# Seven block products in place of eight in the first MLP product of a transformer layer

## The chip, the cores and the metric

The kernel runs on one core of one Trainium2 chip. The metric is the time of one execution on the device in microseconds. The core has five engines with instruction queues of their own: TensorE (PE, matmuls, with its weight loads shown as PEld), VectorE (DVE), ScalarE (ACT), GpSimd (POOL), and SyncE (SP), which here issues all DMAs. SBUF is the memory that the engines work in, PSUM the one that TensorE accumulates in, in eight banks of 512 fp32 columns by 128 partitions.

## The reference

One layer of a diffusion backbone on 512 latent tokens and 256 context tokens of width 1024, in fp32. After two mixers (windowed attention and a gated DeltaNet) and their output projection comes the MLP, and the change is in it:

```python
def mlp(s, shift, scale_m):
    hm = rms_norm(s, g_norm2) * (1.0 + scale_m) + shift
    return jnp.square(jax.nn.relu(hm @ w_mlp1)) @ w_mlp2

x_new = x.astype(jnp.float32) + gt1 * merge(y_attn, o_dl, dz, ga, gd)
x_new = x_new + gt2 * mlp(x_new, sh2, sc2)
```

`w_mlp1` is 1024 x 4096, `w_mlp2` is 4096 x 1024; `hm` has 512 rows (tokens) and 1024 columns.

## The kernel before

Everything is kept transposed: 128 features on the partitions, tokens along the free axis. Each fp32 operand of a matmul is split in two parts of the type fp32r, `hi` (the rounded value) and `lo` (the rest). A product of two such operands takes three matmuls per 128x128 weight block, hi x hi, hi x lo and lo x hi, which `mm3` issues (lines 294, 295, 296). The split is one ACT copy and one DVE subtraction: `split` (lines 182 and 183) for values on the chip, `wload` (lines 240, 245, 246) for weights that it first loads from memory to a `wr` tile (four of them, 512 KB each).

The MLP works in four quarters (`for hf in range(4)`). A quarter computes eight tiles of 128 features of the first product, each from eight 128x128 weight blocks with all 512 tokens as the moving operand (24 matmuls of 512 columns, line 1380), then relu (ACT, line 1382), square (DVE, line 1384) and split (lines 182, 183). Then the second product takes the quarter's eight tiles as its input: for each of eight output tiles 24 matmuls, and DVE adds the gated result to the residual stream `xn_` in SBUF (line 1401). In the last quarter each output tile is stored at once (line 1405). The first three tiles of the first quarter are computed in two halves of 256 tokens, since the norm ahead of the MLP is done by halves (`norm`, `modulate`, lines 299 to 301).

Beside the first quarter's eight tiles the DVE has other work: steps of `late_mod` (lines 1037 to 1042), which load a piece of the modulation weights and reduce it (one instruction of 1024 columns each).

Buffers: `alloc` hands out pieces of one SBUF arena of 167 units of 256 columns in a ring, one after the other, and goes on from where it stopped; `free` returns a piece, and its next owner has to wait until the last reader is done. `keep=True` takes a piece from the top end. Weights of the MLP lie in the arena (`bufs = [alloc(1024), alloc(1024)]`), in the profile `m`; other weights lie in the two rotating pairs of tiles `wh` and `wl`. PSUM banks are handed out by `bank()` in the same way.

A scheduler orders the instructions of each engine when the program is built; it takes the order of the program as a priority and puts a later instruction ahead where an earlier one isn't ready by its own estimate.

Of the kernel before, what the change touches and what calls it, by code (L numbers as in the profile page):

```python
# [11 lines left out]
AF = mybir.ActivationFunctionType  # L12
ALU = mybir.AluOpType
# [17 lines left out]
NPL = ()  # L31
# [3 lines left out]
P = 128  # L35
D = 1024
KT = D // P
# [24 lines left out]
class Buf:  # L62


    def __init__(self, arena, start, n, ap):
        self.arena, self.start, self.n, self.ap = arena, start, n, ap

    def __getitem__(self, k):
        return self.ap[k]

    def free(self):
        for i in range(self.start, self.start + self.n):
# [25 lines left out]
def tile_layer(ctx: ExitStack, tc: tile.TileContext, I: dict, out: bass.AP, dbg=None):  # L98
    nc = tc.nc
    V, A, G, PE = nc.vector, nc.scalar, nc.gpsimd, nc.tensor  # L100
# [19 lines left out]
    alloc, bank = mem.get, lambda n=1: banks.get(n * 512)  # L120
# [10 lines left out]
    r32 = lambda ap: ap.bitcast(F32R)  # L131
    f32_ = lambda ap: ap.bitcast(F32)
# [5 lines left out]
    def act(out_, in_, func, **kw):  # L138

        sets = TABLES.get(func)  # L140
        if sets and actg["set"] not in sets:
            head = A.preload_act_table_set(sets[0])
            for o in actg["ops"]:
                tc.add_manual_dep(head.ins, o.name, nosync, reason="table sets")
            actg.update(set=sets[0], head=head.ins, ops=[head.ins])
        r = A.activation(out_, in_, func, **kw)  # L146
        if sets:
            tc.add_manual_dep(r.ins, actg["head"].name, nosync, reason="table sets")
            actg["ops"].append(r.ins)
        return r  # L150
# [87 lines left out]
    def wload(src, n=KT, bufs=None):  # L238
        raw = sb.tile([P, KT, P], F32, tag="wr", bufs=NWR, name=nm("wr"))[:, :n]
        nc.sync.dma_start(out=raw, in_=src)  # L240
        if bufs:
            hi, lo = (b.ap.rearrange("p (k c) -> p k c", k=KT) for b in bufs)
        else:
            hi, lo = (sb.tile([P, KT, P], F32, tag=t, bufs=NWS, name=nm(t))[:, :n] for t in ("wh", "wl"))
        A.activation(r32(hi), raw, AF.Copy)  # L245
        V.tensor_tensor(r32(lo), raw, hi, op=ALU.subtract)  # L246
        return r32(hi), r32(lo)
# [16 lines left out]
    rx, rc = rstd[:, :512], rstd[:, 512:768]  # L264

    for src, nt, n, r in ((xs_, 4, SEQ, rx), (cs_, 2, CTX, rc)):
        tot = None
        for i in range(nt):
            b = alloc(1024)
# [6 lines left out]
        w = 512  # L276
# [12 lines left out]
    def mm3(acc, w, xs, start=True, stop=True, ks=None):  # L289
        ks = list(range(len(xs))) if ks is None else ks  # L290
        n = len(ks)
        for i, k in enumerate(ks):
            xhi, xlo = xs[i]
            PE.matmul(acc, w[0][:, k, :], xhi, start=(start and i == 0), stop=False)  # L294
            PE.matmul(acc, w[0][:, k, :], xlo, start=False, stop=False)  # L295
            PE.matmul(acc, w[1][:, k, :], xhi, start=False, stop=(stop and i == n - 1))  # L296

    def modulate(t, src, r, sc, sh, hi, lo, eng=V):
        V.scalar_tensor_tensor(t, src, sc, r, op0=ALU.mult, op1=ALU.mult)
        A.activation(r32(hi), t, AF.Identity, bias=sh)  # L300
        eng.scalar_tensor_tensor(r32(lo), t, sh, hi, op0=ALU.add, op1=ALU.subtract)
        return r32(hi), r32(lo)
# [6 lines left out]
    for kt in range(KT):  # L309
        t = alloc(768)  # L310
        o, oc = kt * 1024, kt * 512
# [325 lines left out]
    acc = in_tile(T_AB, True)  # L637
    V.memset(gb[0:64], 0.0)

    t, t2 = alloc(TOK), alloc(TOK)  # L640
# [390 lines left out]
    modT = const.tile([P, 4, 8], F32, name="modT")  # L1031
# [13 lines left out]
    late = (x for grp in range(4) for x in late_mod(grp))  # L1045
# [154 lines left out]
    for g in range(2):  # L1200
        ms = slice(16 * g, 16 * g + 16)
# [11 lines left out]
        for a in range(2):  # L1213
            lo, hi = quad(a, 0), quad(a, 1)
# [36 lines left out]
    for qq in range(2):  # L1251
# [3 lines left out]
        for a in range(2):  # L1255
            n = 2 * qq + a
            t = alloc(512)
# [15 lines left out]
    for ct in range(8):  # L1273
        w = wnext()
# [32 lines left out]
    for ct in range(8 - NHALF):  # L1307
        w = wnext()
# [9 lines left out]
    HM = alloc(8 * 1024, True)  # L1318
    ms = [(r32(HM[:, k * 1024:k * 1024 + 512]), r32(HM[:, k * 1024 + 512:k * 1024 + 1024])) for k in range(KT)]

    wlast = [wnext() for _ in range(NHALF)]
    accs = [bank() for _ in range(NHALF)]
    wfirst = []

    def norm(cols):
# [4 lines left out]
        act(rx[:, cols], rx[:, cols], AF.Exp, scale=-0.5)  # L1330
        for kt in range(KT):
            t = alloc(256)
            modulate(t.ap, xn_[kt][:, cols], rx[:, cols], mA[:, kt:kt + 1], modT[:, 1, kt:kt + 1],
                     f32_(ms[kt][0][:, cols]), f32_(ms[kt][1][:, cols]),
                     G if kt in NPL else V)
            t.free()

    first = []

# [7 lines left out]
    for n, cols in enumerate(halves):  # L1347
        for i in range(NHALF):
            if n and i == NHALF - 1:
                norm(halves[0])  # L1350
            mm3(accs[i][:, cols], wlast[i], cut(ys, cols))
            residual(8 - NHALF + i, accs[i], cols)
    for b in accs:
# [4 lines left out]
        f.append(bank())  # L1358
    for n, cols in enumerate(halves):
        for i, (_, w, acc) in enumerate(first):  # L1360
            mm3(acc[:, cols], w, cut(ms, cols))
            if n == i == 0:
                norm(halves[1])
    for b in [ssq, rx]:
        b.free()
    for b in Y:
        b.free()


    FT = 8  # L1370
    for hf in range(4):
        act_ = []
        for f in range(FT):
            if first:
                bufs, _, acc = first.pop(0)
            else:
                bufs = [alloc(1024), alloc(1024)]
                w = wload(I["wm1"][hf * FT + f], bufs=bufs)
                acc = bank()
                mm3(acc.ap, w, ms)  # L1380
            r, hl = alloc(1024), alloc(1024)
            A.activation(r[:, :512], acc.ap, AF.Relu)
            acc.free()
            V.tensor_tensor(r[:, 512:], r[:, :512], r[:, :512], op=ALU.mult)  # L1384
# [4 lines left out]
            if hf == 0:  # L1389
                next(late)  # L1390
        if hf == 0:
            for _ in late:
                pass
            scr.free()
        xs = [(r32(b[:, :512]), r32(b[:, 512:])) for b in act_]
        for ct in range(8):
            acc = bank()
            bufs = [alloc(1024), alloc(1024)]
            w = wload(I["wm2"][ct * 4 + hf], bufs=bufs)
            mm3(acc.ap, w, xs)  # L1400
            V.scalar_tensor_tensor(xn_[ct], acc.ap, modT[:, 3, ct:ct + 1], xn_[ct], op0=ALU.mult, op1=ALU.add)  # L1401
            for b in bufs + [acc]:
                b.free()
# [112 lines left out]
```

## Time and profile before

| | |
|---|---|
| time, median of 3 runs | 933.06 us (932.63 to 935.54) |
| time of the profiled execution | 930.59 us |
| its span, from the first to the last instruction | 928.8 us |
| TensorE busy | 905.0 us, 97% of the span, 7796 matmuls |
| VectorE busy | 592.6 us, 64% |
| ScalarE busy | 440.6 us, 47% |
| DMA | 98.72 MB, mean 106 GB/s |
| granted TensorE clock | 1.00 throughout |

The profile is one execution as the hardware recorded it. "Busy" is the time in which an engine had an instruction running. Matmuls are pipelined, so the duration of one (0.28 or 0.39 us) is longer than the distance from its start to the next one's start; that distance is what a stream of matmuls costs each. A row of a group gives line, engine, operation, output <- inputs, shapes and count, then the total busy time, the mean duration in ns, and the idle time of the engine just ahead of these instructions with what ended it.

### The profile page before, as it was taken

To read this page: it belongs to the slowest core of one execution; us is meant where nothing else is said; L and a number is where in the kernel's file an instruction comes from. 1 tells how busy PE (TensorE), PEld (TensorE's weight loads), DVE (VectorE), ACT (ScalarE), POOL (GpSimd) and SP (SyncE) were. 2 spreads that over 40 slices of the span, in tenths; PEclk is the share of its full clock that TensorE was granted. 3 is DMA by queue.
4 is the path that set the end of the run, shared out by engine and by line. 5 is a ranking of instruction groups with operands and counts; after the bars stand their busy time and mean duration, and the time that the engine had idled before them with its cause. 6 is when DMAs were issued, how large, how long until landed. Compare 5 with 4: busy or idle time off the path is not lost.

```text
span 928.8 us, 18209 instructions
## 1 busy us (share of the span) xinstructions
PE 905.0 (97%) x7796; PEld 733.7 (79%) x7796; DVE 592.6 (64%) x981; ACT 440.6 (47%) x799; POOL 12.1 (1%) x26
## 2 busy tenths in 40 slices
PE   9999999988999999999999999999999999999998
PEld 7688677867777787778878788988888888888886
DVE  4666799996777997367865978961554235424511
ACT  5467654357567787475554434550253025213400
POOL 0000000000000002000000000000000000000000
PEclk9999999999999999999999999999999999999999
DMA  9911112110000132324524575570444124222111
GB/s 355 371 46 47 48 48 68 48 45 24 24 13 23 58 115 80 106 91 143 177 73 147 173 262 189 158 228 0 141 158 133 59 75 139 92 70 88 45 46 46
DMA packets 29600, 98.72 MB, mean 106 GB/s; under 512 B 3664, under 2 KB 4176, under 8 KB 29520
## 3 DMA queue, kind: packets, MB, share of 16 engines
q1 hardware_dynamic: 29520, 97.57, 31.8%
q8 instruction: 61, 1.00, 0.5%
q14 instruction: 19, 0.16, 0.0%
HBM read 95.46 MB, written 2.10 MB: 105 GB/s over the span
## 4 chain that ended last, share of the span: by engine, by line
PE 72%; DVE 15%; ACT 6%; DMA 4%; issue 2%; SPq 0%; DVEq 0%; ACTq 0%
PE banks L294 16%; PE banks L295 16%; PE banks L296 16%; PE banks L973 10%; DMA wa<-in_wada 2%; DVE wl L246 2%; PE banks L1019 2%; PE banks L1085 2%; ACT m L146 1%; DVE m L803 1%; PE banks L558 1%; DVE m L802 1%; PE banks L1116 1%; PE banks L1097 1%; DVE m L183 1%
## 5 line engine op out<-in xcount | busy, mean ns | idle before, releaser
L294 PE MATMUL banks<-m,m 128*128 128x512 f32 (+1 forms) x584 | 219.0, 378 | 2.0 <-ACT m L300 1.1
L295 PE MATMUL banks<-m,m 128*128 128x512 f32 (+1 forms) x584 | 219.9, 378 | 0.0
L296 PE MATMUL banks<-m,m 128*128 128x512 f32 (+1 forms) x584 | 218.9, 377 | 0.1
L245 ACT ACTIVATE m<-wr 128x1024 fp32r<-128x1024 f32 x67 | 70.9, 1062 | 157.2 <-PE banks L295 78.4
L294 PEld LDWEIGHTS banks<-m,m 128*128 128x128 f32 x584 | 109.0, 188 | 24.7 <-ACT m L300 2.4
L295 PEld LDWEIGHTS banks<-m,m 128*128 128x128 f32 x584 | 109.6, 188 | 22.3 <-issue 1.6
L296 PEld LDWEIGHTS banks<-m,m 128*128 128x128 f32 x584 | 109.5, 188 | 20.8 <-DVE m L246 0.7
L246 DVE TENSOR_TENSOR m<-wr,m 128x1024 fp32r<-128x1024 f32 x67 | 81.5, 1224 | 64.3 <-ACT m L245 35.2
L294 PE MATMUL banks<-m,wh 128*128 128x512 f32 (+1 forms) x312 | 113.6, 365 | 0.8 <-DVE m L1300 0.4
L296 PE MATMUL banks<-m,wl 128*128 128x512 f32 (+1 forms) x312 | 111.2, 359 | 1.5 <-DVE wl L246 1.5
L295 PE MATMUL banks<-m,wh 128*128 128x512 f32 (+1 forms) x312 | 111.0, 356 | 0.0
L973 PE MATMUL banks<-m,wh 128*128 128x512 f32 x320 | 105.0, 402 | 1.3 <-ACT m L146 1.1
L1401 DVE SCALAR_TENSOR_TENSOR m<-banks,modT,m 128x512 f32<-128x512 f32 x32 | 24.0, 750 | 105.4 <-PE banks L296 105.4
L246 DVE TENSOR_TENSOR wl<-wr,wh 128x1024 fp32r<-128x1024 f32 (+1 forms) x60 | 64.7, 1078 | 31.7 <-ACT wh L245 31.5
L245 ACT ACTIVATE wh<-wr 128x1024 fp32r<-128x1024 f32 (+1 forms) x60 | 56.5, 943 | 34.7 <-PE banks L973 14.0
L973 PEld LDWEIGHTS banks<-m,wh 128*128 128x128 f32 x320 | 59.3, 188 | 14.5 <-ACT m L146 1.3
L294 PEld LDWEIGHTS banks<-m,wh 128*128 128x128 f32 x312 | 58.7, 188 | 11.0 <-ACT m L146 0.7
L296 PEld LDWEIGHTS banks<-m,wl 128*128 128x128 f32 x312 | 58.2, 188 | 10.7 <-DVE wl L246 2.2
L973 PE MATMUL banks<-m,wl 128*128 128x512 f32 x160 | 65.7, 411 | 0.0
L295 PEld LDWEIGHTS banks<-m,wh 128*128 128x128 f32 x312 | 58.8, 188 | 8.3 <-issue 0.2
L182 ACT ACTIVATE m<-m 128x512 fp32r<-128x512 f32 (+1 forms) x56 | 35.1, 630 | 46.7 <-DVE m L1384 20.9
L183 DVE TENSOR_TENSOR m<-m,m 128x512 fp32r<-128x512 f32 (+1 forms) x56 | 38.3, 689 | 22.0 <-ACT m L182 21.5
(231 smaller groups left out, 1265.9 us busy)
## 6 DMA issues: line engine op xcount, KB each, us to landing
wr<-in_wm SPq DMA_DIRECT2D x64, 512.0 KB, 3.6
wr<-in_win SPq DMA_DIRECT2D x39, 512.0 KB, 3.7
wa<-in_wada SPq DMA_DIRECT2D x32, 512.0 KB, 4.0
m<-in_wada SPq DMA_DIRECT2D x16, 512.0 KB, 10.2
m<-in_xT SPq DMA_DIRECT2D x8, 512.0 KB, 5.9
wr<-in_wbr SPq DMA_DIRECT2D x16, 256.0 KB, 2.7
wr<-in_wout SPq DMA_DIRECT2D x8, 512.0 KB, 4.5
out<-m SPq DMA_DIRECT2D x8, 256.0 KB, 2.0
```

Of the source, the lines that this page charges most:

```text
L146: r = A.activation(out_, in_, func, **kw)
L182: A.activation(r32(hi), src, AF.Copy)
L183: (eng or V).tensor_tensor(r32(lo), src, hi, op=ALU.subtract)
L245: A.activation(r32(hi), raw, AF.Copy)
L246: V.tensor_tensor(r32(lo), raw, hi, op=ALU.subtract)
L294: PE.matmul(acc, w[0][:, k, :], xhi, start=(start and i == 0), stop=False)
L295: PE.matmul(acc, w[0][:, k, :], xlo, start=False, stop=False)
L296: PE.matmul(acc, w[1][:, k, :], xhi, start=False, stop=(stop and i == n - 1))
L973: PE.matmul(acc.ap, w[x][:, k, :], hx[k][y], start=(k == p == 0), stop=(k == KT - 1 and p == 2))
L1019: PE.matmul(pa.ap, w[x][:, j, :], r32(Q[y][:, :, j, :]), start=(j == p == 0), stop=(j == 3 and p == 2))
L1085: PE.matmul(z[r, x * 256 + q * HD:x * 256 + (q + 1) * HD], src[q][r, col(c):col(c) + CH], S[r, q * HD:(q + 1) * HD], start=True, stop=True)
L1401: V.scalar_tensor_tensor(xn_[ct], acc.ap, modT[:, 3, ct:ct + 1], xn_[ct], op0=ALU.mult, op1=ALU.add)
```

## The change

In quarters two to four the first product is done for two output tiles at once as a product of 2x2 blocks. The moving operand is cut in 2x2 by token half (256) and by feature half (four of the eight column blocks), the weights of the two tiles in 2x2 by feature half and by output tile. Strassen's scheme (the variant with 15 additions) needs seven products of such blocks, where the plain way needs eight. One block product is 4 column blocks x 3 matmuls of 256 columns.

The sums of the activation blocks (S1 to S4) are made once, in `combos` after the first quarter's first product, and split there. The sums of the weight blocks (T1 to T4) are made on the chip for every pair of tiles by DVE and split by ACT and DVE: `load1` makes what the first four products (`first`) need, `load2` what the last three (`second`) need. ACT and DVE put the products together. Relu and square of a pair are now two ACT instructions of 1024 columns.

The activations' layout changes with it: `HM` becomes four kept buffers (by feature half, and hi or lo), and a half of tokens becomes an index in them. `norm` keeps its intermediate `t` (the scaled values ahead of the shift) for `combos`. The second product's weights go to the rotating `wh`/`wl` tiles in place of arena buffers, and its first two output tiles are accumulated together, first over six of the quarter's tiles and then over the last two. The first pair's `load1` and `load2` are issued within the second product of the quarter before, after its fourth and sixth output tile, the second pair's `load1` at that product's end. The first quarter's first product stays as it was, apart from the layout.

```diff
+    class Pair:
+        def parts(self, src, *names):
+            n = src.shape[-1]
+            hi, lo = alloc(n), alloc(n)
+            split(src, hi.ap, lo.ap)
+            for i, w in enumerate(names):
+                self.w[w] = [b.part(i * 512, 512) for b in (hi, lo)]
+
+        def load1(self):
+            raw = [alloc(1024), alloc(1024)]
+            for i, r in enumerate(raw):
+                nc.sync.dma_start(out=r.ap, in_=I["wm1"][self.f + i].rearrange("p k c -> p (k c)"))
+            b11, b21, b12, b22 = [r.part(o, 512) for r in raw for o in (0, 512)]
+            self.parts(b11.ap, "11")
+            t13, t2_ = alloc(1024), alloc(512)
+            V.tensor_tensor(t13[:, :512], b12.ap, b11.ap, op=ALU.subtract)
+            V.tensor_tensor(t2_.ap, b22.ap, t13[:, :512], op=ALU.subtract)
+            self.parts(t2_.ap, "T2")
+            V.tensor_tensor(t13[:, 512:], b22.ap, b12.ap, op=ALU.subtract)
+            self.parts(t13.ap, "T1", "T3")
+            ...
+            self.left = b21, b22, t2_
+
+        def load2(self):
+            b21, b22, t = self.left
+            self.parts(b21.ap, "21")
+            self.parts(b22.ap, "22")
+            V.tensor_tensor(t.ap, b21.ap, t.ap, op=ALU.subtract)
+            self.parts(t.ap, "T4")
+            ...
+
+        def prod(self, dst, x, w):
+            n = 0
+            for k in range(4):
+                for i, j in ((0, 0), (0, 1), (1, 0)):
+                    PE.matmul(dst, r32(self.w[w][i][:, k * P:(k + 1) * P]), xs7[x][k][j], start=(n == 0), stop=(n == 11))
+                    n += 1
+            ...
+
+        def first(self):
+            x, y = bank(), bank()
+            self.o, self.u = alloc(1024), alloc(512)
+            self.prod(x[:, :256], "11", "11")
+            self.prod(x[:, 256:], "S2", "T2")
+            A.activation(self.u.ap, x.ap, AF.Copy)
+            ...
+            V.tensor_tensor(u2, self.u[:, :256], u2, op=ALU.add)
+            self.prod(y[:, :256], "S3", "T3")
+            self.prod(y[:, 256:], "S1", "T1")
+            ...
+            V.tensor_tensor(two(u3), two(y.ap), u2.unsqueeze(1).broadcast_to([P, 2, 256]), op=ALU.add)
+            V.tensor_tensor(self.o[:, 768:], u3[:, :256], y[:, 256:], op=ALU.add)
+
+        def second(self):
+            w, z = bank(), bank()
+            o = self.o
+            self.prod(w[:, :256], "12", "21")
+            V.tensor_tensor(o[:, :256], self.u[:, :256], w[:, :256], op=ALU.add)
+            ...
+            self.prod(z[:, :256], "22", "T4")
+            self.prod(z[:, 256:], "S4", "22")
+            V.tensor_tensor(o[:, 256:768], o[:, 256:768], z.ap, op=ALU.add)
+            A.activation(o.ap, o.ap, AF.Relu)
+            A.activation(o.ap, o.ap, AF.Square)
+            hi, lo = alloc(1024), alloc(1024)
+            split(o.ap, hi.ap, lo.ap)
+            ...
+
+    def combos():
+        t1, t2 = ts
+        sS = [alloc(1024) for _ in range(4)]
+        V.tensor_tensor(sS[2].ap, t1[:, :1024], t2[:, :1024], op=ALU.subtract)
+        V.tensor_tensor(sS[1].ap, t2[:, 1024:], sS[2].ap, op=ALU.subtract)
+        V.tensor_tensor(sS[0].ap, t2[:, :1024], t2[:, 1024:], op=ALU.add)
+        V.tensor_tensor(sS[3].ap, t1[:, 1024:], sS[1].ap, op=ALU.subtract)
+        ...
+        for n, bias in ((1, sh2[:, 4:8]), (2, None), (0, sh1), (3, None)):
+            hi, lo = AS[n][:, :1024], AS[n][:, 1024:]
+            if bias is None:
+                split(sS[n].ap, hi, lo)
+            else:
+                for k in range(4):
+                    c = slice(k * 256, k * 256 + 256)
+                    A.activation(r32(hi[:, c]), sS[n][:, c], AF.Identity, bias=bias[:, k:k + 1])
+                    V.scalar_tensor_tensor(r32(lo[:, c]), sS[n][:, c], bias[:, k:k + 1], hi[:, c], op0=ALU.add, op1=ALU.subtract)
+        ...
     for hf in range(4):
-        for f in range(FT):
+        for f in range(0 if hf else FT):
...
         if hf == 0:
+            xs7 = combos()
...
+        w2 = lambda ct: wload(I["wm2"][ct * 4 + hf])
+        ps_ = pairs[hf]
+        for i, p_ in enumerate(ps_):
+            p_.first()
+            if i:
+                p_.load2()
+            if i + 1 < len(ps_):
+                p_.second()
+            if i + 2 < len(ps_):
+                ps_[i + 2].load1()
+        ws = [w2(0), w2(1)]
+        if hf:
+            ps_[-1].second()
+        accs = [bank(), bank()]
+        ks = list(range(FT))
+        for cols in (ks[:FT - 2], ks[FT - 2:]):
+            for acc, w in zip(accs, ws):
+                mm3(acc.ap, w, [xs[k] for k in cols], start=(cols[0] == 0), stop=(cols[-1] == FT - 1), ks=cols)
         for ct in range(8):
-            acc = bank()
-            bufs = [alloc(1024), alloc(1024)]
-            w = wload(I["wm2"][ct * 4 + hf], bufs=bufs)
-            mm3(acc.ap, w, xs)
+            if ct > 1:
+                accs.append(bank())
+                mm3(accs[ct].ap, w2(ct), xs)
...
+            if hf < 3 and ct in (3, 5):
+                (pairs[hf + 1][0].load1 if ct == 3 else pairs[hf + 1][0].load2)()
...
+        if hf < 3:
+            pairs[hf + 1][1].load1()
```

More of the change, by code (lines that the diff above doesn't have):

```diff
@@ L69, in __getitem__, with part @@
         return self.ap[k]
+    def part(self, o, cols):
+        u = self.arena.unit
+        return Buf(self.arena, self.start + o // u, cols // u, self.ap[:, o:o + cols])
     def free(self):
@@ new lines, in combos @@
+    def combos():
[5 more added lines that the diff above has]
+        V.tensor_tensor(sS[3].ap, t1[:, 1024:], sS[1].ap, op=ALU.subtract)
+        for b in ts:
+            b.free()
+        sh1 = small([P, 4], "sh1", bufs=1)
+        sh2 = modT[:, 1]
+        V.tensor_tensor(sh1, sh2[:, 0:4], sh2[:, 4:8], op=ALU.add)
+        AS = [alloc(2048, True) for _ in range(4)]
+        quarter = lambda ap: ap.rearrange("p (k t) -> p k t", k=4)
+        for n, bias in ((1, sh2[:, 4:8]), (2, None), (0, sh1), (3, None)):
[7 more added lines that the diff above has]
+                    V.scalar_tensor_tensor(r32(lo[:, c]), sS[n][:, c], bias[:, k:k + 1], hi[:, c], op0=ALU.add, op1=ALU.subtract)
+        for b in sS:
+            b.free()
+        xs7 = {"11": mh[0][:4], "12": mh[0][4:], "22": mh[1][4:]}
+        for n in range(4):
+            hi, lo = quarter(r32(AS[n][:, :1024])), quarter(r32(AS[n][:, 1024:]))
+            xs7[f"S{n + 1}"] = [(hi[:, k], lo[:, k]) for k in range(4)]
+        return xs7
@@ L1370, in tile_layer @@
     FT = 8
+    pairs = [[Pair(hf * FT + f) for f in range(0, FT, 2)] if hf else [] for hf in range(4)]
     for hf in range(4):
-        act_ = []
-        for f in range(FT):
+        act_, xs = [], []
+        for f in range(0 if hf else FT):
             if first:
```

60 lines of the change are left out of this document (41 added, 19 removed).

## The prediction, made before the changed kernel ran

> **What bounds the kernel now.** I read the page first (engine shares, slices, the chain that ended last), then busy time by stretches of the MLP, then the timeline for the distance from one matmul's start to the next, and last the groups by shape for the duration of each kind of instruction.
>
> ```profile
> span 928.8 us, 18209 instructions
> PE 905.0 (97%) x7796; PEld 733.7 (79%) x7796; DVE 592.6 (64%) x981; ACT 440.6 (47%) x799; POOL 12.1 (1%) x26
> DVE  4666799996777997367865978961554235424511
> PEclk9999999999999999999999999999999999999999
> PE 72%; DVE 15%; ACT 6%; DMA 4%; issue 2%; SPq 0%; DVEq 0%; ACTq 0%
> ```
>
> TensorE (PE) is busy 97% of the span and carries 72% of the chain; VectorE (DVE) is busy 64%, but unevenly: up to nine tenths in the middle, two to four tenths at the end, where the MLP runs. The granted clock never falls.
>
> ```profile
> 600.00:620.00 20.00, 20.00 (x90) 16.57 (x89) 17.50 (x22) 12.43 (x15) 0.00 (x0) 1.00 0.81 262
> 700.00:780.00 80.00, 80.00 (x354) 66.29 (x353) 31.89 (x36) 23.53 (x29) 0.00 (x0) 1.00 0.29 92
> ```
>
> The columns are PE, weight loads, DVE, ACT and POOL busy, then clock, DMA share and GB/s. From the second quarter of the MLP on, PE never pauses: 80.00 of 80.00 us, while DVE has 31.89 and ACT 23.53. So here the time is the number of matmuls times the distance between their starts, and whatever shortens that column shortens the kernel, until another engine takes its place.
>
> ```profile
> 581.95 0.28 PE L295 MATMUL banks<-m,m 128*128 128x256 f32 x1
> 583.87 0.28 PE L296 MATMUL banks<-m,m 128*128 128x256 f32 x1
> 594.24 0.39 PE L294 MATMUL banks<-m,m 128*128 128x512 f32 x1
> 599.00 0.39 PE L294 MATMUL banks<-m,m 128*128 128x512 f32 x1
> 519.85 0.23 PE banks L294
> 526.15 0.23 PE banks L294
> ```
>
> The first two rows are 16 matmuls apart: a 256-column matmul costs 1.92/16 = 0.120 us. The next two are 21 apart: 512 columns cost 4.76/21 = 0.2267 us. The last two (from the chain) are 27 apart, in the output projection: 512 columns cost 6.30/27 = 0.2333 us there. That stage differs in one thing that matters below: its weights lie in the rotating tiles `wh`/`wl`, those of the MLP in the arena (`m`).
>
> **The PE term.** A pair of output tiles of the first MLP product takes 2 x 8 x 3 = 48 matmuls of 512 columns: 48 x 0.2267 = 10.88 us. The change takes 7 products x 4 x 3 = 84 matmuls of 256 columns: 84 x 0.120 = 10.08 us. An eighth fewer columns gives only 7%, because a narrow matmul costs more per column. There are 12 such pairs in quarters two to four: 12 x 0.80 = 9.6 us gained, if PE never waits.
>
> [...]
>
> **The DVE term.** This is what the gain has to pay for.
>
> ```profile
> L246 DVE TENSOR_TENSOR m<-wr,m 128x1024 fp32r<-128x1024 f32 x64 | 77.9, 1224 | 64.3 <-ACT m L245 35.2 <-PE banks L295 27.1 <-PE banks L296 0.8
> L183 DVE TENSOR_TENSOR m<-m,m 128x512 fp32r<-128x512 f32 x36 | 24.8, 691 | 20.4 <-ACT m L182 20.3
> L1384 DVE TENSOR_TENSOR m<-m 128x512 f32<-128x512 f32 x32 | 21.9, 686 | 7.0 <-ACT m L1382 7.0
> L1304 DVE TENSOR_TENSOR m<-m,m 128x256 f32<-128x256 f32 x6 | 2.5, 418 | 0.0
> L1401 DVE SCALAR_TENSOR_TENSOR m<-banks,modT,m 128x512 f32<-128x512 f32 x32 | 24.0, 750 | 105.4 <-PE banks L296 105.4
> L245 ACT ACTIVATE m<-wr 128x1024 fp32r<-128x1024 f32 x64 | 67.8, 1062 | 157.2 <-PE banks L295 78.4 <-PE banks L296 58.7 <-DMA wr<-in_wm 12.9
> L182 ACT ACTIVATE m<-m 128x512 fp32r<-128x512 f32 x36 | 22.6, 630 | 28.3 <-DVE m L1384 20.9 <-DVE m L1280 6.3
> L1382 ACT ACTIVATE m<-banks 128x512 f32<-128x512 f32 x32 | 18.8, 590 | 21.9 <-PE banks L296 21.9
> ```
>
> Per pair before: DVE 2 x (1.22 + 0.69 + 0.69) = 5.2 us beside 10.88 of PE. After, by the same rows: `load1` has three differences and two splits of 512 and one split of 1024, 5 x 0.69 + 1.22 = 4.67; `load2` one difference and three splits, 2.76; `first` 0.42 + 0.69 + 0.42 = 1.53; `second` 0.42 + 0.69 + 1.22 = 2.33. Together 11.29 us, more than the 10.08 of PE beside it. ACT: five splits of 0.63, one of 1.06, a copy of 0.59, and relu, square and split of 1.06 each: 7.98, so it fits.
>
> So DVE would set the time of this stage if all of it were done there. It isn't: `load1` and `load2` of a quarter's first pair (7.43) are issued during the second product before it, where DVE has 1.22 + 0.75 = 1.97 us per output tile against 24 x 0.2267 = 5.44 of PE, an idle 3.47 x 8 = 27.8. What stays in a stage is 4 x 11.29 - 7.43 = 37.7, and two `wh`/`wl` splits of the second product, 2.4: 40.1 us of DVE beside 4 x 10.08 = 40.3 of PE. Back to back, four 1024-splits took less than their durations:
>
> ```profile
> 664.24 4.62 DVE L246 TENSOR_TENSOR m<-wr,m 128x1024 fp32r<-128x1024 f32 x4
> ```
>
> 4.62 against 4.90, so 40.1 may shrink to 37.8. The two engines are level, and what counts is who waits where.
>
> **Where PE waits.** I walked the third quarter, with t = 0 at its first product. The order on each engine isn't the program's: in 600 to 620 the trace has weight splits for the second product ahead of squares of the first. I assumed that the earliest instruction in the program whose inputs and buffer are ready goes first. Buffers come from the ring `alloc`; I followed its allocations by hand to see whose place each takes.
>
> ```profile
> wr<-in_wm SPq DMA_DIRECT2D x64, 512.0 KB, 3.6
> ```
>
> The raw weights of pair 1 lie over activations that the last output tile of the second quarter reads until t = -1.4; with 3.6 us to land they arrive at 2.2, and its `load1` runs on ACT and DVE in turn until about 8.6, in time for its first product at 10.1. On SP, loads behind this one wait with it; they are those of later pairs, whose places aren't free earlier. Then `load1` of pair 2 stands before `load2` of pair 1 in the program, so from about t = 9 DVE has it (4.67), the end of pair 0's `second` (0.69 + 1.22), pair 1's `first` (1.53) and pair 1's `load2` (2.76): 10.9 by durations, 10.2 at the back-to-back rate. T4 closes that list, at 19.2, or at 18.6 if one split of `load2` fits in a gap before; I take 18.9. PE's turn for the `lo` half of T4 comes five products and two matmuls after 10.1, at 10.1 + 5 x 1.44 + 0.24 = 17.5, so it waits 1.4. After that `load2` of pair 2 is ready some 3 us early. In the second quarter pair 1's data wait for nothing so late, in the fourth they land at -0.5: no such wait. In each quarter a piece of pair 3's `load2` lies over T1 or T3 of its own `first`, and can be written only when that has ended: one split of 0.69 less two matmuls, 0.5 us. Sum 1.4 + 3 x 0.5 = 2.9 us lost.
>
> **What is at nothing, with its cover.** Relu, square and split of the last pair (0.69 + 3 x 1.06 + 1.22 and hand-overs, 5.6 us) lie behind 36 matmuls that two output tiles do on the first six column blocks, 8.2 us; without them the 5.6 would be bare. The second product's weights move from arena buffers to two `wh`/`wl` pairs: a split (1.06 + 1.22) can start when the tile before last is done and has 5.44 us; uncovered it would cost 2.3 per tile. The combinations `combos` take DVE 6 x 1.22 + 8 x 0.48 = 11.2 us in the first quarter, whose eight tiles load it with 8 x (1.22 + 0.69 + 0.69 + 1.22) = 30.6 of 43.5, and which no longer splits second-product weights far ahead; I price what spills into the second product at 0.5, between 0 and the 2.4 of two weight splits.
>
> ```profile
> L301 DVE SCALAR_TENSOR_TENSOR m<-m,modT,m 128x256 fp32r<-128x256 f32 x16 | 7.0, 482 | 0.1
> L1039 DVE SCALAR_TENSOR_TENSOR m<-wa,m 128x1024 f32<-128x1024 f32 x16 | 19.4, 1220 | 2.8 <-DMA wa<-in_wada 1.5 <-PE banks L296 1.2
> ```
>
> **The second product's pitch** is the unknown. Its weights move to `wh`/`wl`; if that is what makes 0.2333 of 0.2267, it costs 4 x 8 x 24 x 0.0066 = 5.1 us; a gain has no row for it. The moving operand, the stage and the neighbours stay those of the 0.2267 rows, so I take 0 and keep 5.1 as the bound.
>
> **Sum**: -9.6 + 2.9 + 0.5 + 0 = -6.2 us. The profiled execution took 930.59 (span 928.8 and 1.8 around it), so 924.4 there; the median of the runs shown, 933.06, is 2.5 above it, which makes 926.9.
>
> **Rivals.** *Pitch by place* (0.2): the 5.1 us are paid, and the gain is 1.1, so 931.9: no change that can be told. For it: every long stretch on `wh`/`wl` outside the MLP stands near 0.233. Against it: nothing ties the number to the weights rather than to the stage.
>
> *DVE takes over* (0.28, slower): between `load1` of pair 1 and `load2` of pair 3 a stage has 3 x 4.67 + 3 x 2.76 + 4 x 1.53 + 3 x 2.33 = 35.4 us of DVE. It splits values that ACT has just rounded, turn by turn. At the share that it reached in 600 to 620, 17.50/20 = 0.875, that lasts 40.5; with 2.2 before and two products, 2.9, behind it a stage takes 45.6 against 4 x 10.88 = 43.5 before, so 3 x 2.1 + 0.5 = 6.8 slower, 939.9. It decides from a share below 35.4/(43.5 - 5.1) = 0.92. Against it: a list that fills gaps with later work, and the wide idle DVE of the second product.
>
> *No waits* (0.05): DVE keeps ahead; 9.6 gained, 923.5.
>
> *Weight loads set the narrow matmul's pace* (0.02).
>
> ```profile
> L296 PEld LDWEIGHTS banks<-m,m 128*128 128x128 f32 x536 | 100.6, 188 | 18.9
> ```
>
> A weight load lasts 188 ns. If they didn't overlap, 84 x 0.188 = 15.8 us per pair, 4.9 more than now, 59 us in all: 992. The 0.120 rows, each with its own load, speak against it. [...]
>
> **Chances.** The forecast has 0.45. Faster by over 0.3% (2.8 us, about what a measurement here can tell from nothing): 0.45 of it and of *no waits* less a little, and the better edge of *pitch by place*: 0.53. Within 0.3%: most of *pitch by place*, 0.15. Slower: *DVE takes over*, weight loads, and stalls past my walk: 0.32. The range goes from 922.5, just under *no waits*, to 939.5, inside *DVE takes over*, which leaves about 0.2 out. The likeliest case's own range is 923.5 to 930.
>
> **What would show it.** The starts of matmuls in `prod` 0.120 apart, and in the second product 0.2267 or 0.2333. Each first product of quarters two to four 41 to 42 us long, not 43.5 or 45; DVE's share in it near 0.9. PE's waits there few, in the third quarter on a DVE split of T4 in pair 1, and about 0.5 us at the start of `second` of pair 3. Wrong would be a wait of PE on DVE in every pair, a pause of PE before the first quarter's second product, or a lower granted clock.

## The result: no change that can be told

The changed kernel took 934.14 us (median of 12 runs, 930.84 to 936.89), the kernel before 933.03 us (12 runs, 931.01 to 935.54) on the same chip. The ratio is 1.0006, with a 95% interval from 0.9992 to 1.0021. The profiled execution of the changed kernel took 930.84 us, 0.25 more than that of before; it is the fastest of its 12 and lies 3.3 below their median, as before's lies 2.4 below its own, so the two profiles can be set side by side.

The page of the changed kernel, by the same rows as before:

```profile
span 929.1 us, 19276 instructions
...
PE 903.2 (97%) x8228; PEld 747.0 (80%) x8228; DVE 665.0 (72%) x1116; ACT 482.7 (52%) x857; POOL 12.0 (1%) x26
```

PE has 432 matmuls more and is busy as long as before, and DVE has 72 us more. The second quarter in two stretches, first and second product, of before and then of after (columns as in the prediction: PE, weight loads, DVE, ACT and POOL busy, clock, DMA share, GB/s):

```profile
663.57:707.09 43.52, 43.52 (x193) 35.84 (x192) 27.83 (x30) 22.82 (x29) 0.00 (x0) 1.00 0.56 181
707.09:750.75 43.66, 43.66 (x194) 36.19 (x193) 13.81 (x15) 7.41 (x9) 0.00 (x0) 1.00 0.27 85
```
```profile
665.52:705.65 40.13, 40.13 (x332) 39.85 (x331) 32.02 (x49) 22.89 (x32) 0.00 (x0) 1.00 0.24 80
705.65:751.25 45.60, 45.60 (x200) 36.57 (x198) 23.26 (x29) 14.16 (x17) 0.00 (x0) 1.00 0.32 105
```

The granted clock is full in both. The first product is 3.4 us shorter, the second 1.9 longer; 0.6 of the 1.9 are five matmuls of the next quarter's first product that run within it. What became of the distance between starts, in the timeline of PE after:

```profile
671.75 18.46 PE L1427 MATMUL banks<-m,m 128*128 128x256 f32 x152
...
718.35 0.39 PE L299 MATMUL banks<-m,wh 128*128 128x512 f32 x1
...
721.85 0.40 PE L299 MATMUL banks<-m,wh 128*128 128x512 f32 x1
```

The products of 256 columns (L1427) stand (18.46 - 0.28)/151 = 0.120 us apart, as forecast. The last two rows are 15 starts apart: 3.50/15 = 0.2333, where before the second product had 0.2267. On PE a quarter ends with the last matmul of its second product (line 296 before, 301 after); these rows, before and then after, are the ends of the four quarters:

```profile
663.14 0.39 PE L296 MATMUL banks<-m,m 128*128 128x512 f32 x1
...
750.32 0.39 PE L296 MATMUL banks<-m,m 128*128 128x512 f32 x1
...
837.36 0.39 PE L296 MATMUL banks<-m,m 128*128 128x512 f32 x1
...
924.40 0.39 PE L296 MATMUL banks<-m,m 128*128 128x512 f32 x1
```
```profile
665.29 0.39 PE L301 MATMUL banks<-m,wl 128*128 128x512 f32 x1
...
751.02 0.39 PE L301 MATMUL banks<-m,wl 128*128 128x512 f32 x1
...
836.95 0.39 PE L301 MATMUL banks<-m,wl 128*128 128x512 f32 x1
...
924.82 0.39 PE L301 MATMUL banks<-m,wl 128*128 128x512 f32 x1
```

The first quarter ends 2.15 us later. The others last 85.7, 85.9 and 87.9 us against 87.2 and twice 87.0: a gain of 1.5, a gain of 1.1 and a loss of 0.8. With 4 x 10.08 + 8 x 24 x 0.2333 a quarter without pauses would be 85.1. So the second loses 0.6 us, the third 0.8 and the fourth 2.8 to pauses of PE, and those show most fully as waits of its weight loads (MLP alone, before and then after):

```profile
PEld banks L294 <- ACT m L300: 1.6, 2, 1.3
PEld banks L294 <- ACT m L245: 0.3, 1, 0.3
PEld banks L295 <- DVE m L301: 0.2, 1, 0.2
```
```profile
PEld banks L299 <- ACT m L305: 1.4, 1, 1.4
PEld banks L301 <- DVE wl L251: 1.3, 2, 0.7
PEld banks L1427 <- DVE m L188: 1.2, 3, 0.7
PEld banks L1427 <- DMA m<-in_wm: 0.9, 1, 0.9
...
```

The columns are total, times and longest; left out are a row of 0.3 and three of 0.2. The first row of each is mainly a wait for the norm ahead of the MLP. The sum went from 2.1 to 5.7 us: splits of products' weights (L188), of the second product's weights (L251), and raw weights still on their way (DMA).

My theory at this point: the second product pays about 5.1 us for the place of its weights, and the rest of the gain goes to waits. The rival: DVE's 72 us of new work make the waits and the place is a side matter.

### The profile page after: what moved, and what is told of

Same layout as the page of the kernel before. It is cut to its first block, busy times and chain, and to the rows that moved or that the text cites. A ratio compares the mean times of both kernels' runs of the same rounds, so it can differ in the third digit from the quotient of the medians.

```text
span 929.1 us, 19276 instructions
## 1 busy us (share of the span) xinstructions
PE 903.2 (97%) x8228; PEld 747.0 (80%) x8228; DVE 665.0 (72%) x1116; ACT 482.7 (52%) x857; POOL 12.0 (1%) x26
## 4 chain that ended last, share of the span: by engine, by line
PE 72%; DVE 15%; ACT 6%; DMA 4%; issue 2%; ACTq 0%; DVEq 0%
PE banks L299 12%; PE banks L300 12%; PE banks L301 12%; PE banks L1427 11%; PE banks L978 10%; DVE wl L251 2%; PE banks L1024 2%; PE banks L1090 2%; ACT m L151 2%; DMA wa<-in_wada 1%; DMA m<-in_wm 1%; DVE m L188 1%; PE banks L193 1%; PE banks L563 1%; PE banks L1121 1%
## 5 line engine op out<-in xcount | busy, mean ns | idle before, releaser
L299 PE MATMUL banks<-m,wh 128*128 128x512 f32 (+1 forms) x568 | 214.6, 379 | 0.5 <-ACT wh L250 0.2
L301 PE MATMUL banks<-m,wl 128*128 128x512 f32 (+1 forms) x568 | 212.5, 376 | 2.1 <-DVE wl L251 2.1
L300 PE MATMUL banks<-m,wh 128*128 128x512 f32 (+1 forms) x568 | 212.1, 374 | 0.0
L251 DVE TENSOR_TENSOR wl<-wr,wh 128x1024 fp32r<-128x1024 f32 (+1 forms) x92 | 103.7, 1128 | 34.2 <-ACT wh L250 31.7
L1427 PE MATMUL banks<-m,m 128*128 128x256 f32 x1008 | 124.0, 284 | 1.5 <-DMA m<-in_wm 0.7
L301 PEld LDWEIGHTS banks<-m,wl 128*128 128x128 f32 x568 | 106.2, 188 | 23.6 <-DVE wl L251 3.5
L1427 PEld LDWEIGHTS banks<-m,m 128*128 128x128 f32 x1008 | 122.2, 192 | 3.5 <-DVE m L188 1.2
L299 PEld LDWEIGHTS banks<-m,wh 128*128 128x128 f32 x568 | 106.6, 188 | 22.5 <-ACT wh L250 0.9
L300 PEld LDWEIGHTS banks<-m,wh 128*128 128x128 f32 x568 | 106.7, 188 | 19.8 <-issue 0.2
L187 ACT ACTIVATE m<-m 128x512 fp32r<-128x512 f32 (+2 forms) x118 | 82.3, 720 | 76.2 <-DVE m L1285 12.8
L188 DVE TENSOR_TENSOR m<-m,m 128x512 fp32r<-128x512 f32 (+2 forms) x118 | 92.4, 804 | 22.0 <-ACT m L187 17.0
L1554 DVE SCALAR_TENSOR_TENSOR m<-banks,modT,m 128x512 f32<-128x512 f32 x32 | 24.0, 749 | 85.7 <-PE banks L301 85.7
L978 PEld LDWEIGHTS banks<-m,wh 128*128 128x128 f32 x320 | 59.2, 188 | 14.4 <-ACT m L151 1.3
L299 PE MATMUL banks<-m,m 128*128 128x256 f32 (+1 forms) x136 | 44.5, 342 | 2.0 <-ACT m L305 1.2
L1044 DVE SCALAR_TENSOR_TENSOR m<-wa,m 128x1024 f32<-128x1024 f32 x32 | 38.9, 1219 | 10.4 <-DMA wa<-in_wada 10.3
L300 PE MATMUL banks<-m,m 128*128 128x256 f32 (+1 forms) x136 | 45.4, 341 | 0.0
L301 PE MATMUL banks<-m,m 128*128 128x256 f32 (+1 forms) x136 | 44.5, 336 | 0.1
L978 PEld LDWEIGHTS banks<-m,wl 128*128 128x128 f32 x160 | 30.0, 188 | 7.0
```

Source lines behind the costliest of these rows:

```text
L187: A.activation(r32(hi), src, AF.Copy)
L188: (eng or V).tensor_tensor(r32(lo), src, hi, op=ALU.subtract)
L978: PE.matmul(acc.ap, w[x][:, k, :], hx[k][y], start=(k == p == 0), stop=(k == KT - 1 and p == 2))
L1044: V.scalar_tensor_tensor(t.ap, wa, 0.5, scr.ap, op0=ALU.mult, op1=ALU.mult, accum_out=modT[:, grp, j:j + 1])
L1427: PE.matmul(dst, r32(self.w[w][i][:, k * P:(k + 1) * P]), xs7[x][k][j], start=(n == 0), stop=(n == 11))
L1554: V.scalar_tensor_tensor(xn_[ct], accs[ct].ap, modT[:, 3, ct:ct + 1], xn_[ct], op0=ALU.mult, op1=ALU.add)
```

## The experiments

Two inserted lines shift the line numbers of some kernels by two (L1427 is then L1429, L299 to L301 are L301 to L303). An unchanged kernel before ran beside each; it stood at 933.2 to 933.5.

**Is it the place, and what of the place?** Four kernels. In `after_skew32` and `before_skew32` a tile of 32 bytes per partition, not otherwise used, stands between the pools:

```diff
+    skew = ctx.enter_context(tc.tile_pool(name="skew", bufs=1))
     sb = ctx.enter_context(tc.tile_pool(name="sb", bufs=1))
+    V.memset(skew.tile([P, 8], F32, name="skew"), 0.0)
```

> The changed kernel with nothing but an unused tile of 32 bytes per partition put between two pools, so that the weight tiles wh and wl start 32 bytes further on: from byte 32 of a 64-byte line to byte 0 of one, where every buffer of the arena starts. Theory 'alignment': the distance between 512-column matmuls depends on where in a 64-byte line the weights start; the second product goes from 0.2333 to 0.2267 us, 768 x 0.0067 = 5.1 us gained there, and the stages ahead of the MLP that use wh and wl (some 1080 matmuls of 512 columns) gain up to 7 us more where PE sets their time, less up to 1 us for 256-column ones (0.117 to 0.120): 5 to 11 us faster than the changed kernel. Theory 'region': what counts is that wh and wl lie above the arena (beyond 192 KB); all stays as it is, 0.2333 and no gain. Theory 'rotation': what counts is that two pairs of tiles are written and read in turn; also no gain.

Measured: 927.14, ratio 0.9928 [0.9914, 0.9942]. The same matmuls, the same tiles, moved by 32 bytes:

```profile
715.84 0.39 PE L303 MATMUL banks<-m,wl 128*128 128x512 f32 x1
...
718.56 0.39 PE L303 MATMUL banks<-m,wl 128*128 128x512 f32 x1
```

They are 12 starts apart: 2.72/12 = 0.2267. So neither the tiles nor the stage make 0.2333, but the address. (The waits of the weight loads in the MLP aren't the same in this run: 8.6 us in place of 5.7.)

> The kernel before the change with the same 32 bytes put in. Its MLP uses the arena alone, so this shows what the stages ahead of the MLP are worth. Alignment: up to 7 us faster (1080 matmuls x 0.0067) as far as PE sets the time of those stages, less 336 x 0.003 = 1 us; I expect 3 to 6. Region, rotation: the same as before.

Measured: 931.76, ratio 0.9986 [0.9975, 0.9998], a gain of 1.3 (0.2 to 2.3). In the output projection the wide matmuls on `wh`/`wl` now start 0.227 apart, and PE is busy for 903.2 us in place of 905.0, yet the stages ahead of the MLP give only that. My 3 to 6 was too much; that PE doesn't set the time in them throughout would explain it, but wasn't tested. `after_skew32` gained 7.0 on the changed kernel by the medians and 3.9 by the two profiled spans (929.1 and 925.2), of which the first belongs to that kernel's fastest execution. The 5.1 of the second product and these 1.3, less the 2.9 by which the waits grew, are 3.5, which fits the spans and not the medians. So this account closes only to the 3 us by which the two comparisons differ.

`after_w2_arena` puts the second product's weights back in arena buffers:

```diff
-        w2 = lambda ct: wload(I["wm2"][ct * 4 + hf])
+        wb = {}
+        def w2(ct):
+            wb[ct] = [alloc(1024), alloc(1024)]
+            return wload(I["wm2"][ct * 4 + hf], bufs=wb[ct])
...
-            accs[ct].free()
+            for b in wb.pop(ct) + [accs[ct]]:
+                b.free()
```

> The changed kernel with the second product's weights in arena buffers again, as before the change, with all else of the change kept. All theories of the pitch (alignment, region, rotation): the second product at 0.2267 us per matmul again, 5.1 us gained against the changed kernel, so about 5 us faster than before the change, within 1.5 us, because the ring hands out other places and PE's small waits move. Rival 'the stage': the pitch belongs to the seven-product scheme's surroundings (busier DVE and ACT); then it stays at 0.2333 and nothing is gained.

Measured: 925.01, ratio 0.9916 [0.9894, 0.9938], 9.1 under the changed kernel. That is 4 more than the distance is worth: in its trace the waits of the weight loads in the MLP are 2.7 us in place of 5.7, and the profiled spans differ by 8.0 (929.1 and 921.1), which is 5.1 + 3.0 within 0.1. `before_w2_pool` is the reverse, done to the kernel before:

```diff
-            bufs = [alloc(1024), alloc(1024)]
-            w = wload(I["wm2"][ct * 4 + hf], bufs=bufs)
+            w = wload(I["wm2"][ct * 4 + hf])
...
-            for b in bufs + [acc]:
-                b.free()
+            acc.free()
```

> The kernel before the change, with one thing of the change done alone: the second product's weights go to wh and wl. If the place of the weights is the whole loss: second product at 0.2333 us, 5.1 us slower than before. If the loss comes from the scheme's surroundings: same as before. A wait for the two rotating pairs would show as pauses of PE between output tiles and more than 5.1 us.

Measured: 936.96, ratio 1.0038 [1.0023, 1.0053], so 3.5 slower (2.1 to 4.9), with the starts 0.2333 apart. The profiled spans (934.2 and 928.8, both at a clock of 1.00) differ by 5.4. So this one step of the change costs, by itself, most of the 5.1 or all of it.

**What about the address?** `probe_offsets` measures it alone:

```diff
+    pw, px = act_[0].ap, HM.ap
+    pb = bank()
+    for q in range(24):
+        PE.matmul(pb[:, :512], r32(pw[:, 1 + q % 3 * 128:129 + q % 3 * 128]), r32(px[:, 0:512]), start=(q == 0), stop=(q == 23))
+    pb.free()
...
```

> The kernel before with 24 groups of 24 matmuls at its end, whose result nobody reads: weights at byte offsets 0, 4, 8, 16, 32, 48, 64 and 96 within the lines, for 512 and 256 columns, then the moving operand at bytes 32 and 16, then 128 columns. Alignment to 64 bytes: 0.2267 at offsets 0 and 64, 0.2333 at 32 and 96, for 512 columns; 0.120 and 0.117 for 256; the moving operand's offset changes nothing. If the rule were alignment to 32 bytes, 16 and 48 would be slow and 32 not. Region: all offsets alike at 0.2267.

A group's length less one matmul's own, over 23 (22 where a record is missing), is the distance. In order: 512 columns with the weights 0 and 4 bytes off, the moving operand at 0; the moving operand 32 bytes off with weights 0 and 32 off; 256 columns with weights 0 and 64 off:

```profile
927.74 5.38 PE L1412 MATMUL banks<-m,m 128*128 128x512 f32 x23
932.97 5.74 PE L1416 MATMUL banks<-m,m 128*128 128x512 f32 x24
...
972.07 5.75 PE L1444 MATMUL banks<-m,m 128*128 128x512 f32 x24
977.65 5.61 PE L1448 MATMUL banks<-m,m 128*128 128x512 f32 x24
...
988.67 3.03 PE L1456 MATMUL banks<-m,m 128*128 128x256 f32 x24
...
1005.66 2.89 PE L1480 MATMUL banks<-m,m 128*128 128x256 f32 x24
```

The first is (5.38 - 0.39)/22 = 0.2268, the next two 0.2326 and 0.2330, and with both operands 32 bytes off 0.2270 again: in these groups it is the difference of the two addresses that counts, not the place of either. At 256 columns the order is the reverse, 0.1196 with no difference and 0.1135 with 64 bytes.

`all_skew32` moves the arena too, so that the difference stays as in the changed kernel:

```diff
+    nc.alloc_sbuf_tensor("skew", [P, 8], F32, side="left")
+    base += 32
     nc.alloc_sbuf_tensor("arena", [P, NU * 256], F32, side="left")
```

> The changed kernel with 32 unused bytes ahead of the arena, so that everything moves by 32: arena buffers, activations among them, start at byte 32 of a 64-byte line, wh and wl at byte 0. It reverses which weights lie where. Theory 'alignment of the weights': narrow matmuls of the products (weights in the arena) at 0.117 in place of 0.120, 1008 x 0.003 = 3.0 us gained against after_skew32; second product at 0.2267 although its moving operand is now at byte 32; the first quarter's first product (weights in the arena) at 0.2333, 0.8 us lost; in sum about 925. Rival 'alignment of the moving operand': the second product stays at 0.2333 and the time near 934.

Measured: 934.99, ratio 1.0012 [0.9997, 1.0027], with the second product's starts 0.2333 apart. Alignment of the weights alone, which I had expected to give 925, fell. The time fits the rival in the expectation too, alignment of the moving operand, but not so the probe, where moving both operands by 32 bytes gave 0.2270; the difference stands.

`probe_periods` is the same probe with other offsets.

> The kernel before with 24 groups of 24 matmuls at its end, 12 of 512 columns and 12 of 256, whose weights and moving operand start at chosen byte offsets (weights 0, 64, 128, 192, 256, 320, 512 with the moving operand at 0; weights 0 with moving 64 and 192; both at 64; weights 80 and 96 with moving 0); the groups' results go nowhere. If the distance of two starts depends on the difference of the two start addresses with a period of 128 bytes, 512 columns take 226.7 ns at differences 0, 128, 256 and 512 and about 233 at 64, 192 and 320, and 256 columns about 119.5 at the former and 113.5 at the latter. With a period of 256 bytes the difference of 128 goes with the slow ones at 512 columns. With 512, 256 does too.

Here the rows are 512 columns with the weights 0, 64, 128, 192, 256, 320 and 512 bytes off and the moving operand at 0, then the moving operand 64 bytes off with weights 0; and 256 columns with weights 64 off and moving 0, and weights 0 and moving 192 off:

```profile
928.78 5.60 PE L1412 MATMUL banks<-m,m 128*128 128x512 f32 x24
934.22 5.76 PE L1416 MATMUL banks<-m,m 128*128 128x512 f32 x24
939.82 5.74 PE L1420 MATMUL banks<-m,m 128*128 128x512 f32 x24
945.39 5.67 PE L1424 MATMUL banks<-m,m 128*128 128x512 f32 x24
950.90 5.61 PE L1428 MATMUL banks<-m,m 128*128 128x512 f32 x24
956.35 5.76 PE L1432 MATMUL banks<-m,m 128*128 128x512 f32 x24
961.95 5.63 PE L1436 MATMUL banks<-m,m 128*128 128x512 f32 x24
967.42 5.68 PE L1440 MATMUL banks<-m,m 128*128 128x512 f32 x24
...
998.04 2.99 PE L1464 MATMUL banks<-m,m 128*128 128x256 f32 x24
...
1020.82 2.89 PE L1496 MATMUL banks<-m,m 128*128 128x256 f32 x24
```

Differences of 0 to 256 give 0.2265, 0.2335, 0.2326, 0.2296 and 0.2270, those of 320 and 512 again 0.2335 and 0.2278. The moving operand 64 bytes on is a difference of -64, and gives 0.2300, the value of 192: at the differences tried the period is 256 bytes; of the expectation's three cases the second. The 64-byte lines of the expectations were a guess of mine that no run shows. As the programs are built, `wh` begins in the changed kernel at byte 211296 of a partition and the arena at 16512, a difference of 224 modulo 256; the 32 bytes made it 0. For 256 columns the difference isn't the whole story: of the last two rows, both with a difference of 64 modulo 256, one gives 0.1178 and the other 0.1135. Nor are the two addresses: the first of these rows has the operands at the very places that gave 0.1135 in `probe_offsets`.

**Who makes the waits?** `no_weight_sums` leaves the weight sums out: T1 to T4 are split from raw blocks, so four DVE subtractions per pair are gone, and the output is another.

```diff
-            V.tensor_tensor(t13[:, :512], b12.ap, b11.ap, op=ALU.subtract)
-            V.tensor_tensor(t2_.ap, b22.ap, t13[:, :512], op=ALU.subtract)
-            self.parts(t2_.ap, "T2")
-            V.tensor_tensor(t13[:, 512:], b22.ap, b12.ap, op=ALU.subtract)
-            self.parts(t13.ap, "T1", "T3")
+            self.parts(b22.ap, "T2")
+            self.parts(raw[1].ap, "T1", "T3")
...
-            V.tensor_tensor(t.ap, b21.ap, t.ap, op=ALU.subtract)
-            self.parts(t.ap, "T4")
+            self.parts(b21.ap, "T4")
```

> The changed kernel without the sums of weight blocks: T1 to T4 are split from raw blocks, so four DVE subtractions of 512 columns per pair are left out (12 x 2.76 = 33 us of DVE), everything else and all buffers' places kept. Theory 'DVE sets PE's waits in quarters three and four' (4.2 us of pauses beyond the pitch in the profile of the changed kernel): most of the pauses go, 2.5 to 4 us faster than the changed kernel. Rival 'places': the pauses come from buffers that become free late, and the DMA behind them; they stay, under 1.5 us gained.

Measured: 933.22, ratio 0.9999 [0.9986, 1.0012], 0.9 under the changed kernel.

```profile
PE 903.5 (97%) x8228; PEld 746.7 (80%) x8228; DVE 636.7 (68%) x1068; ACT 483.3 (52%) x857; POOL 12.0 (1%) x26
```

DVE has 28.3 us less to do than in the changed kernel, and nearly nothing comes of it: the waits of the weight loads in the MLP are 6.1 us, in place of 5.7. The rival falls: it isn't these 28 us of DVE's work that make PE wait. That late buffers do, the other theory of the expectation, is what is left, and isn't shown by this run.

`arena_and_skew` has both mends, the 32 bytes and the second product's weights in the arena.

> The changed kernel with both steps: the second product's weights in arena buffers and the 32 unused bytes ahead of wh and wl, so that every weight in the kernel starts at byte 0 of a 64-byte line. Theory 'alignment': the two gains are for different matmuls and add up: 9.1 of the arena step less nothing, and 1.5 that the skew brought to the kernel before, so about 923.5. Rival 'one gain seen twice' (both steps only repair the second product): 925.0 as with the arena step alone.

Measured: 922.58, ratio 0.9889 [0.987, 0.9907]: the best version, 10.4 us (8.7 to 12.1) faster than the kernel before. That is nearer to the 923.5 of two gains than to the 925.0 of one, though the intervals of this kernel and of `after_w2_arena` overlap. The ends of its first three quarters, and the waits of its weight loads in the MLP (from 572 us on, so that the wait for the norm is in it as above):

```profile
661.75 0.39 PE L303 MATMUL banks<-m,m 128*128 128x512 f32 x1
...
746.41 0.39 PE L303 MATMUL banks<-m,m 128*128 128x512 f32 x1
...
830.76 0.39 PE L303 MATMUL banks<-m,m 128*128 128x512 f32 x1
```
```profile
PEld banks L301 <- ACT m L307: 1.4, 1, 1.4
PEld banks L1429 <- ACT m L1465: 0.5, 2, 0.3
PEld banks L1429 <- DVE m L1443: 0.5, 1, 0.5
PEld banks L1429 <- DVE m L190: 0.4, 2, 0.2
...
```

Left out are two rows of 0.2. A quarter lasts 84.7 and 84.4, near the 4 x 10.08 + 43.5 = 83.8 without a pause, and the waits are 3.2 us in place of 5.7, with nearly the same DVE work. On the changed kernel the gain is 11.6 by the medians: 5.1 of distance, 1.3 of the stages ahead of the MLP and 2.5 of waits are 8.9 together. By the profiled spans (929.1 and 919.3) it is 9.8. The rest has no row. The waits fall with the arena step (`after_w2_arena` has 2.7) and not with the 32 bytes (`after_skew32` has 8.6). What differs in that step is which buffers the ring hands out when, and that the second product's weights no longer alternate between two pairs of tiles; which of the two did more was not tried apart.

**Can the narrow matmuls be made faster too?** `narrow_shift` is `arena_and_skew` with the kept buffers of S1 to S4 put 64 bytes before a unit:

```diff
-        AS = [alloc(2048, True) for _ in range(4)]
+        AS = [alloc(2304, True)[:, 240:2288] for _ in range(4)]
```

> arena_and_skew (second product's weights in the arena, the wh and wl tiles moved by 32 bytes) with one more edit: the four kept buffers of S1 to S4 are taken one unit larger and used from column 240 on, so that the weights of their products start 64 bytes after the moving operand, modulo 1 KB. The first product's matmuls of 256 columns on S1 to S4 are 12 pairs x 4 products x 12 = 576. If the distance of two starts follows the difference of the addresses, as in the probe's 113.4 against 119.4 ns at 256 columns, they stand 0.113 to 0.114 apart where those on HM stay at 0.120, and the time falls by 576 x 0.006 = 3.5 us from arena_and_skew's 922.6, to 919.1. If the narrow distance in the kernel is not set by the addresses, or if DVE or the buffers' places take back what PE gains (four units less in the ring), the time stays at 922 to 925.

Measured: 938.28, ratio 1.0051 [1.0033, 1.0069]: 15.7 slower than `arena_and_skew`, outside both expectations. The distance itself did what I expected. These are undisturbed stretches at the start of the third quarter, first of `arena_and_skew` and then of `narrow_shift`:

```profile
746.64 13.60 PE L1429 MATMUL banks<-m,m 128*128 128x256 f32 x112
```
```profile
750.74 10.29 PE L1429 MATMUL banks<-m,m 128*128 128x256 f32 x87
```

They give (13.60 - 0.28)/111 = 0.120 and (10.29 - 0.28)/86 = 0.1164. Counted off by products in the trace, the matmuls on S1 to S4 mostly stand 0.114 apart and those on `HM` 0.118 to 0.120. But PE waited. Its waits in the MLP, of which `arena_and_skew` has the third (1.2, for the norm) and 0.3 us besides:

```profile
PE banks L1429 <- ACT m L189: 7.8, 7, 2.0
PE banks L1429 <- DVE m L190: 3.1, 4, 1.2
PE banks L301 <- ACT m L307: 1.2, 1, 1.2
...
```

The splits that PE waits for came late because ACT waited for raw weights. In the groups by shape from 655 us on, the 512-column splits of `arena_and_skew` and then of `narrow_shift`:

```profile
L189 ACT ACTIVATE m<-m 128x512 fp32r<-128x512 f32 x54 | 33.2, 627 | 59.6 <-PE banks L303 20.8 <-PE banks L302 16.8 <-PE banks L1429 6.9
```
```profile
L189 ACT ACTIVATE m<-m 128x512 fp32r<-128x512 f32 x55 | 33.2, 624 | 73.8 <-DMA m<-in_wm 36.0 <-PE banks L303 14.4 <-PE banks L1429 10.6
```

The largest part of ACT's idle time ahead of them, 36.0 of 73.8 us, is now ended by the DMA of the weights. The edit takes four units from the ring and moves the places of all that follow, so places for the loads come free later; that link is argued from the allocator, the lateness itself is in the rows. And around 766 us the pauses cost more than their length:

```profile
764.00:768.00 4.00, 1.26 (x8) 0.85 (x7) 3.85 (x6) 3.83 (x5) 0.00 (x0) 0.86 0.00 0
768.00:774.00 6.00, 6.00 (x30) 6.00 (x30) 2.42 (x4) 0.34 (x1) 0.00 (x0) 0.53 0.00 0
```

After 4 us with PE busy for 1.26, the granted clock was 0.53 for the next 6, an estimated 6 x 0.47 = 2.8 us lost. What narrow distances would bring in a kernel without these waits stays open.

## Why the prediction was wrong, by its steps

**The second product's pitch** is the step that failed. I had both figures, 0.2267 and 0.2333, and named the weights' place as what differs, and took 0 of the 5.1 us because nothing tied the number to the weights rather than to the stage. Nothing excluded it either, so the 0 was a guess. The 32 bytes tie the number to the place: the second product had its 0.2333, 5.1 us. The rival *pitch by place* was the outcome in its mechanism and its verdict, no change that can be told; its 931.9 against 934.14 has the waits too small. Its name was right only by half, since the cause isn't a kind of buffer but the difference of two addresses.

**The PE term** held: 0.120 between narrow starts. The first products of quarters two to four take 40.1, 40.6 and 42.5 us in the trace, against 4 x 10.08 = 40.3 without a pause; up to five matmuls of each run in the quarter before.

**The waits** were too small in the sum and in other places than those I walked: 2.9 and 0.5 for `combos` against a remainder of 0.3 + 9.6 - 5.1 = 4.8 in the spans. The weight loads' rows show 3.6 of it, the 5.7 less the 2.1 of before; 1.2 has no row. What the walk named hardly came: counted off in the trace, PE pauses 0.2 us on T4 of pair 1 in the third quarter, where I had 1.4, and 0.2 to 0.3 in pair 3 of each quarter, where I had 0.5. That the total came near 3.4 is then luck. I had no wait for a late load in the fourth quarter; the two longest pauses of the first products are there:

```profile
851.60 1.59 PE L1427 MATMUL banks<-m,m 128*128 128x256 f32 x11 [0.54 <-DVE m L188]
...
861.63 1.57 PE L1427 MATMUL banks<-m,m 128*128 128x256 f32 x11 [0.66 <-DMA m<-in_wm]
```

**DVE takes over** didn't happen. In the first product of the second quarter DVE is busy 32.02 of 40.13 us, 0.80 and not 0.9, and 28 us less of its work changed the time by 0.9, within the noise. (For the kernel before I read two to four tenths of DVE at the end; its slices there show one to five. The sum doesn't use it.) **No waits** came close to true for the version with the mends, not for the change as made. **Weight loads set the pace** didn't happen either: 0.120 with a load for each.

With the two terms put right the sum is -9.6 + 4.8 + 5.1 = +0.3, the difference of the spans; it closes because 4.8 is what was left over, and with the measured 3.6 it is -0.9. The forecast of 926.9 was 7.2 us too low: 5.1 is the pitch, 1.4 the waits, and 0.7 lies between profiles and medians. With the 32 bytes the changed kernel took 927.14, close to the forecast by luck: it has 6.5 us more waits than the kernel before where the forecast had 3.4, and 1.3 from stages that the forecast left alone.

## What to carry to other kernels

When an edit moves an operand to another buffer, look up the distance between starts of the same matmul in both places, and if a row shows two values, price the edit by the row of the new place until something is known that excludes it. Where a stream of wide matmuls (512 columns here) is the bound, compare the addresses of weights and moving operand modulo 256 bytes: in the two probes equal ones gave 0.2265 to 0.228 us between starts and the others up to 0.234, and 32 bytes of padding gave 7 us here by the medians. An edit that moves buffers or work in time can move the waits by as much as the step itself is worth (here the weight loads' 5.7 us became 2.7 in one version and 8.6 in another), so look at them after each such edit.

## What the runs showed of the hardware that I had not expected

The distance between two matmuls of 512 columns (fp32r, a weight load each) is 0.2265 to 0.228 us in the two probes when weights and moving operand start at the same byte modulo 256, and 0.230 to 0.234 at the other differences tried; at 256 columns it is 0.119 to 0.120 when they do, and 0.113 to 0.120 otherwise, by a rule that I have not found. What in the hardware makes the 3% between 0.2265 and 0.2335 isn't shown.

In `narrow_shift` two pauses within 4 us, in which PE was busy for 1.26 us and the longest wait was 2.0 us, were followed by a clock of 0.53 for 6 us. From 868 to 872 us PE was busy for 1.59 us, and the clock was 0.66 in the next 5 us. A single pause of 1.9 us at 678.89 us had nothing of the kind after it: from 664 to 688 us PE is busy for 22.09 of the 24 us and the clock is 1.00. What in the pauses brings the clock down isn't shown.
